# The per-layer gate of a one-layer encoder by Strassen's algorithm on token rows, with its weight operands kept on chip

## The chip, the cores and the metric

The kernel runs on one core of one Trainium2 chip. The metric is device time in microseconds (us) of that core: 2111.22 us before the change, the median of three runs that lie between 2110.23 and 2114.58 us.

## The reference

One layer of a streaming encoder, 2048 tokens of width 1024, all float32. The part that the change touches is the last two lines; `h` is the layer-normalised sum of input and token mixer, `p` a second input of width 256.

```
h = layer_norm(ALPHA * h + mix, ln1_g, ln1_b)
f = (silu(h @ ffn_w1) * (h @ ffn_w3)) @ ffn_w2          # width 2816
r = ALPHA * h + f
e = (p @ ple_w) * sigmoid(r @ ple_gate_w)               # "gate" and "ple"
out = layer_norm(r + e, ln2_g, ln2_b)
```

`ple_gate_w` is 1024 by 1024, `ple_w` is 256 by 1024, ALPHA is 2 to the power 1/4.

## The kernel before, in words

Every float32 product is made of three TensorE matmuls on operands cut in a high and a low part: `split` (L99 to L102) rounds a tile into its high part on ScalarE (ACT) and subtracts it for the low part on VectorE (DVE), and `mm3` (L122 to L125) issues high by high, high by low, low by high into one PSUM bank of 128 by 512. There are eight such banks, handed out in turn by `anybank`.

The stages follow one another: input projection, state-space scan and pooling, output projection and first layer norm (to about 519 us in the trace), then for each half `h` of the tokens (1024 tokens) `w13(h)`, which makes the SwiGLU's two products, and `w2_half(h)`, which makes `f` transposed, features on the partitions. At the end comes the gate over four blocks of 512 tokens, two in each half.

`w13` and `w2_half` use Strassen's algorithm in Winograd's form: a block product of 2 by 2 quadrants in seven products instead of eight. `weights7` (L770) loads two weight pieces, forms four sums on DVE and yields seven split operands one at a time; `next_w` (L819) takes them from a stream that runs five operands ahead (`LEAD`), over six buffers. The other side's seven operands are made once by `pieces7` (L823), written to DRAM (`Xv`, `Gv`) and read back by the GpSimd (POOL) queue into tiles that stay in SBUF (`xload1` for `w13(1)`, tile `xv`; `load_g` for `w2_half`, tile `gv`). `product` (L910) adds each of the seven into one of three banks, and the kernel reads a bank out between two products, by an ACT copy or a DVE add.

In `w2_half` the sums of six groups of such products collect in eight tiles `HR`: four copies by ACT in the first group (L1011), DVE adds elsewhere (L1012). After the last group ACT's queue writes them to DRAM as `Rr` (L1044), 16 transfers for each half.

The gate before does without Strassen. `prep_r` (L1047) reads `Rr` (tile `rr`) and `h` (tile `hn`, from `Hn`), adds ALPHA times `h` on DVE (L1056) and splits the sum into `rT`. `gate` does three of the four blocks with features on the partitions: for each of eight feature tiles two products for ple (bank `eb`) and eight for the gate (bank `ab`), with the weights streamed in and split for every block; `ln2` then transposes the result on TensorE (bank `vb`), normalises and writes it. The last block goes through `gate_rows`: tokens on the rows, the transposed `r` in `ro`, the same number of matmuls.

The program's order on each engine is fixed when the kernel is built: a scheduler walks the program by priority and hands out tile buffers as they come free, so instructions of neighbouring stages lie interleaved on an engine. Each engine then works its list strictly in order. DMAs are issued in order as well, from the lists of SP, ACT and POOL.

Of the kernel before, what the change touches and what calls it, by code (L numbers as in the profile page):

```python
# [40 lines left out]
def trunk_kernel(  # L41
# [125 lines left out]
    Gv = drp.tile([2, NF // 2, 7, 128, 1024], F32, name="Gv")  # L167
    Rr = drp.tile([2, 2, 128, 8, 512], F32, name="Rr")
# [599 lines left out]
    def weights7(src_a, src_b, pairs, sums=sums_x):  # L768
# [13 lines left out]
        a11, a12 = load(src_a)  # L782
        yield one(a11)
        a21, a22 = load(src_b)
# [189 lines left out]
    def w2_half(h):  # L974

        after = latest[0]
# [16 lines left out]
        for gi, pairs in W2:  # L993
# [53 lines left out]
    def prep_r(h, q):  # L1047

        rT[h][q], HR[h][q] = [], []
        for m2 in range(4):  # L1050
            t = slot([128, 2, 512], "rr")
            G.dma_start(t, Rr[h, q, :, 2 * m2:2 * m2 + 2])
            hn = sbig([128, 2, 512], "hn")
            for m in range(2):
                G.dma_start(hn[:, m], Hn[h, 2 * m2 + m, :, q])
            V.scalar_tensor_tensor(t, hn, ALPHA, t, MUL, ADD)  # L1056
            for m in range(2):
                HR[h][q].append(t[:, m])
                pr = pair("rT")
                split(pr[:, 0], pr[:, 1], t[:, m])  # L1060
                rT[h][q].append(pr)
            yield

    def prep_p(h, q):
        pr_ = xp.tile([128, 2, 512], F32, tag="x", name="pr_")
        SP.dma_start(pr_, pt[h, q].rearrange("p (k s) -> p k s", k=2))
        pT[h][q] = []
        for k in range(2):
            pr = pair("pT", sp)
            split(pr[:, 0], pr[:, 1], pr_[:, k])  # L1070
            pT[h][q].append(pr)

    def gate(h, q, banks=6):
        for m in range(8):
            if m % 4 == 0:
                ph, pl = weight(ple_w[m // 4], 2, 512)
            wh, wl = weight(gate_w[m], 8, 128)
            ms = slice(128 * (m % 4), 128 * (m % 4) + 128)
            ab, eb = anybank("ab", banks), anybank("eb", banks)
            for k in range(2):  # L1080
                mm3(eb, ph[:, k, ms], pl[:, k, ms], pT[h][q][k][:, 0], pT[h][q][k][:, 1], k == 0, k == 1)
            for k in range(8):
                mm3(ab, wh[:, k], wl[:, k], rT[h][q][k][:, 0], rT[h][q][k][:, 1], k == 0, k == 7)
            sg = evp.tile([128, 512], F32, tag="ev", name="sg")
            A.activation(sg, ab, AF.Sigmoid)
            V.tensor_tensor(sg, sg, eb, MUL)
            V.tensor_tensor(HR[h][q][m], HR[h][q][m], sg, ADD)
            yield

    def vtrans(b, h, q, t, m2):  # L1090
        for m in range(4):
            PE.transpose(b[:, m], HR[h][q][4 * m2 + m][:, 128 * t:128 * t + 128], ident)
        return b.rearrange("p a b -> p (a b)")


    ro = []

    def rows_r(h, q):

        two = slp.tile([128, 2, D], F32, tag="sl", name="ro")  # L1100
        ro.extend([two[:, 0], two[:, 1]] + [sbig([128, D], "ro") for _ in range(2)])
        for t in range(4):
            for m2 in range(2):
                A.copy(ro[t][:, 512 * m2:512 * m2 + 512], vtrans(tbank([128, 4, 128], "va"), h, q, t, m2))
            yield

    def weight2(src):

        raw = rawp[0].tile([128, 2, 512], F32, tag="wr", name="wr")
        SP.dma_start(raw, src.rearrange("p (k n) -> p k n", k=2))  # L1110
        wh, wl = pair("wh2"), pair("wl2")
        split(wh, wl, raw)
        return wh, wl

    def gate_rows(h, q):
        st = [sm.tile([128, 2, 6], F32, tag="st", name="st") for _ in range(4)]
        for n in range(2):
            ns = slice(512 * n, 512 * n + 512)
            acc = [bank([128, 512], "ab") for _ in range(4)]

            def part(t, us, kk0):
                cs = slice(128 * t, 128 * t + 128)
                for i, (wh, wl) in enumerate(us):
                    for k in range(2):
                        kt = 2 * (kk0 + i) + k
                        rp = rT[h][q][kt]
                        mm3(acc[t], rp[:, 0, cs], rp[:, 1, cs], wh[:, k], wl[:, k], kt == 0, kt == 7)

            for kk in range(2):
                u = weight(gate_r[n, kk], 2, 512)  # L1130
                for t in range(4):
                    part(t, [u], kk)
                yield
            ph, pl = weight2(ple_w[n])
            if n == 0:
                us = [weight(gate_r[n, kk], 2, 512) for kk in (2, 3)]
            else:
                us = [weight2(gate_r[n, kk]) for kk in (2, 3)]
            for t in range(4):
                cs = slice(128 * t, 128 * t + 128)  # L1140
                eb = side([128, 512], "eb")
                for k in range(2):
                    pp2 = pT[h][q][k]
                    mm3(eb, pp2[:, 0, cs], pp2[:, 1, cs], ph[:, k], pl[:, k], k == 0, k == 1)
                part(t, us, 2)
                sg = evp.tile([128, 512], F32, tag="ev", name="sg")
                A.activation(sg, acc[t], AF.Sigmoid)
                V.tensor_tensor(sg, sg, eb, MUL)
                V.tensor_tensor(ro[t][:, ns], ro[t][:, ns], sg, ADD)
                V.bn_stats(st[t][:, n], ro[t][:, ns])  # L1150
                if n == 1:
                    mv, rstd = ln_scale(st[t])
                    nb = sm.tile([128, 1], F32, tag="nb", name="nb")
                    V.scalar_tensor_tensor(nb, mv[:, 0:1], -1.0, rstd, MUL, MUL)
                    cut_at = CUTS[t]
                    o0, o1 = ro[t][:, 0:cut_at], ro[t][:, cut_at:D]
                    A.activation(o1, o1, AF.Identity, bias=nb, scale=rstd)
                    V.scalar_tensor_tensor(o0, o0, mv[:, 0:1], g2b[:, 0, 0:cut_at], SUB, MUL)
                    V.scalar_tensor_tensor(o0, o0, rstd, g2b[:, 1, 0:cut_at], MUL, ADD)
                    G.tensor_tensor(o1, o1, g2b[:, 0, cut_at:D], MUL)  # L1160
                    G.tensor_tensor(o1, o1, g2b[:, 1, cut_at:D], ADD)
                    SP.dma_start(ov[h, 4 * q + t, :, 0:cut_at], o0)
                    SP.dma_start(ov[h, 4 * q + t, :, cut_at:D], o1)
                yield

    def ln2(h, q):
        for t in range(4):
            bs = [vtrans(tbank([128, 4, 128], "vb"), h, q, t, m2) for m2 in range(2)]
            mv, rstd = ln_stats(bs)
            o = xp.tile([128, D], F32, tag="x", name="o")  # L1170
            for m2 in range(2):
                ms = slice(512 * m2, 512 * m2 + 512)
                V.scalar_tensor_tensor(o[:, ms], bs[m2], mv[:, 0:1], g2b[:, 0, ms], SUB, MUL)
            V.scalar_tensor_tensor(o, o, rstd, g2b[:, 1], MUL, ADD)
            G.dma_start(ov[h, 4 * q + t], o)
            yield
# [41 lines left out]
    rT, HR, pT = ([[None, None], [None, None]] for _ in range(3))  # L1218

# [24 lines left out]
    drive(w13(1), None, 0)  # L1244
    drive(w2_half(1), None, 0)
    mid_pools.close()
    rawp[0] = ctx.enter_context(tc.tile_pool(name="wrq", bufs=2, reuse_waits="tile"))
    g2b = slp.tile([128, 2, D], F32, tag="sl", name="g2b")
    G.dma_start(g2b[:, 0], ln2_g.broadcast_to([128, D]))
# [81 lines left out]
```

## Time and profile before

| What | Value |
|---|---|
| median of three runs | 2111.22 us |
| the profiled execution, its own time | 2113.13 us |
| its span, first to last instruction | 2111.4 us |
| mean granted TensorE clock | 0.987 |
| PE (matmul) busy | 2031.3 us, 96% |
| DVE busy | 1582.4 us, 75% |
| ACT busy | 858.1 us, 41% |
| POOL busy | 333.1 us, 16% |

The span is 1.7 us shorter than the execution's own time, and that execution is 1.9 us above the median. Matmuls overlap each other in the record, so a single one is recorded longer than the step from one to the next; the cost of one more matmul is read from a stretch in which TensorE never waits, as time by count. Idle time of an engine that is not the bottleneck costs nothing. In the trace's lists "idle before" an instruction names what released it.

### The profile page before, as it was taken

Reading aid. Unit: us, or ns where it says so; the run is one execution under the profiler, and the core shown is the slowest. Engines: PE = TensorE matmul, PEld = TensorE weight load, DVE = VectorE, ACT = ScalarE, POOL = GpSimd, SP = SyncE. Lnnn points to the kernel's source line nnn. Section 1 sums busy time; section 2 is a strip of 40 time slices with the busy share of each in tenths; the row PEclk is TensorE's granted clock in tenths of the full one; section 3 lists DMA queues with packets and bytes.
Section 4 is the critical chain, followed back from the end, with each engine's and each line's share of the span. In section 5 each row is a group of like instructions: output and inputs, shape, how many; then the busy total and the mean of one; then the engine's idle time right before and its main releaser. Section 6 shows DMA issues by size and latency. Waiting matters only on the chain.

```text
span 2111.4 us, 25700 instructions
## 1 busy us (share of the span) xinstructions
PE 2031.3 (96%) x9064; PEld 1644.9 (78%) x9064; DVE 1582.4 (75%) x2812; ACT 858.1 (41%) x1453; POOL 333.1 (16%) x603
## 2 busy tenths in 40 slices
PE   9999899999899999999999999999999899979997
PEld 7877678777688778887788888888888688758886
DVE  7599699668688786666788867767766588866877
ACT  4533645644555454344222244444434322142341
POOL 2012101110111111013211100101103221111113
PEclk9999999999999999999999999999999999989999
DMA  7636757766656654349766833434438876354542
GB/s 250 219 119 210 275 169 235 233 213 216 219 211 245 246 216 165 124 176 398 284 248 227 301 140 134 171 134 150 169 130 342 315 262 237 129 220 148 207 164 100
DMA packets 149184, 440.82 MB, mean 209 GB/s; under 512 B 15344, under 2 KB 41552, under 8 KB 149056
## 3 DMA queue, kind: packets, MB, share of 16 engines
q0 software_dynamic: 72160, 258.80, 32.9%
q1 hardware_dynamic: 42912, 148.92, 20.2%
q10 hardware_dynamic: 33984, 31.46, 4.3%
q8 instruction: 71, 1.16, 0.2%
q14 instruction: 57, 0.47, 0.1%
HBM read 292.88 MB, written 148.34 MB: 209 GB/s over the span
## 4 chain that ended last, share of the span: by engine, by line
PE 71%; DMA 10%; issue 7%; DVE 7%; ACT 3%; POOL 2%; SPq 0%; POOLq 0%; ACTq 0%; DVEq 0%
PE fb L123 12%; PE fb L125 12%; PE fb L124 12%; PE f L123 6%; PE f L125 6%; PE f L124 6%; PE ab L123 2%; PE ab L124 2%; PE ib L125 2%; PE ab L125 2%; PE ib L123 2%; PE ib L124 2%; DMA hl<-Hd 1%; DMA gv<-Gv 1%; DMA Hd<-ze 1%
## 5 line engine op out<-in xcount | busy, mean ns | idle before, releaser
L123 PE MATMUL fb<-xv,wv 128*128 128x512 f32 x1232 | 482.2, 396 | 6.4 <-ACT u L961 4.5
L124 PE MATMUL fb<-xv,wv 128*128 128x512 f32 x1232 | 486.0, 394 | 0.0
L125 PE MATMUL fb<-xv,wv 128*128 128x512 f32 x1232 | 482.3, 395 | 0.2 <-DVE wv L102 0.2
L101 ACT CAST wv<-ws 128x512 fp32r<-128x512 f32 x264 | 163.6, 620 | 379.1 <-PE fb L125 179.9
L123 PEld LDWEIGHTS fb<-xv,wv 128*128 128x128 f32 x1232 | 232.3, 189 | 61.3 <-ACT u L961 6.1
L125 PEld LDWEIGHTS fb<-xv,wv 128*128 128x128 f32 x1232 | 232.1, 188 | 54.6 <-DVE wv L102 0.6
L124 PEld LDWEIGHTS fb<-xv,wv 128*128 128x128 f32 x1232 | 232.5, 189 | 53.0
L123 PE MATMUL f<-gv,wv 128*128 128x512 f32 x616 | 242.3, 397 | 15.9 <-ACT HR L1011 13.6
L1012 DVE TENSOR_TENSOR HR<-HR,f 128x512 f32<-128x512 f32 x304 | 202.7, 684 | 60.2 <-PE f L125 56.5
L124 PE MATMUL f<-gv,wv 128*128 128x512 f32 x616 | 243.5, 395 | 0.0
L102 DVE TENSOR_TENSOR wv<-ws,wv 128x512 fp32r<-128x512 f32 x264 | 181.6, 688 | 81.8 <-ACT wv L101 81.4
L125 PE MATMUL f<-gv,wv 128*128 128x512 f32 x616 | 235.5, 395 | 0.0
L101 ACT CAST wh<-wr 128x1024 fp32r<-128x1024 f32 (+1 forms) x102 | 101.6, 999 | 219.3 <-PE ab L124 73.7
L831 POOL DMA_DIRECT2D Gv<-xo x154 | 82.7, 537 | 660.7 <-DVE xo L102 625.6
L102 DVE TENSOR_TENSOR wl<-wr,wh 128x1024 fp32r<-128x1024 f32 (+1 forms) x102 | 117.8, 1158 | 71.0 <-ACT wh L101 70.9
L101 ACT CAST wv<-wq 128x512 fp32r<-128x512 f32 x198 | 122.5, 621 | 90.0 <-PE f L125 65.3
L102 DVE TENSOR_TENSOR wv<-wq,wv 128x512 fp32r<-128x512 f32 x198 | 136.0, 687 | 30.2 <-ACT wv L101 29.1
L123 PEld LDWEIGHTS f<-gv,wv 128*128 128x128 f32 x616 | 116.6, 189 | 45.7 <-ACT HR L1011 14.9
L124 PEld LDWEIGHTS f<-gv,wv 128*128 128x128 f32 x616 | 116.7, 189 | 26.5
L125 PEld LDWEIGHTS f<-gv,wv 128*128 128x128 f32 x616 | 116.4, 189 | 26.9
L989 POOL DMA_DIRECT2D gv<-Gv x154 | 81.6, 531 | 230.2 <-PE f L125 187.8
L101 ACT CAST xo<-tt 128x512 fp32r<-128x512 f32 x104 | 64.6, 621 | 111.7 <-DVE tt L844 62.4
(316 smaller groups left out, 3563.4 us busy)
## 6 DMA issues: line engine op xcount, KB each, us to landing
Gv<-xo POOLq DMA_DIRECT2D x154, 512.0 KB, 3.1
gv<-Gv POOLq DMA_DIRECT2D x154, 512.0 KB, 7.5
wq<-in_w_dram SPq DMA_DIRECT2D x132, 512.0 KB, 4.2
wr<-in_w_out_dram SPq DMA_DIRECT2D x32, 512.0 KB, 4.4
Xv<-xo POOLq DMA_DIRECT2D x28, 512.0 KB, 3.8
xv<-Xv POOLq DMA_DIRECT2D x28, 512.0 KB, 5.9
wr<-in_gate_w_dram SPq DMA_DIRECT2D x24, 512.0 KB, 4.0
pre<-in_x_dram SPq DMA_DIRECT2D x16, 512.0 KB, 5.7
```

What stands on the lines that cost most here:

```text
L101: A.copy(hi, src)
L102: V.tensor_tensor(lo, src, hi.bitcast(F32), SUB)
L123: PE.matmul(ps, ah, bh, start=first, stop=False, **kw)
L124: PE.matmul(ps, ah, bl, start=False, stop=False, **kw)
L125: PE.matmul(ps, al, bh, start=False, stop=last, **kw)
L831: G.dma_start(dst[i], v.bitcast(F32).rearrange("p a n -> p (a n)"))
L989: G.dma_start(v.bitcast(F32).rearrange("p a n -> p (a n)"), Gv[h, pi, i])
L1012: return V.tensor_tensor(o, o, bank, ADD)
```

## The change

The gate is done by Strassen for all tokens, as eight pairs of 128-token tiles (`PAIRS`), tokens on the rows.

- `w2_half` reads `h` (tile `hl`) from SP's queue and adds ALPHA times it to `HR[um]` on DVE, once for each of the eight tiles, in groups 1 to 4 of the six (two in each). `Rr` then holds `r` itself, and `prep_r` goes.
- `wprep` runs beside `w13(1)`: it loads `gate_r` (eight SP transfers, tile `gw`), forms the seven operands of the gate's weights with `pieces7` and writes them to `Wv`. `wload` reads all 28 back on POOL's queue after `w2_half(1)`'s last weight load, into the places that `xv` had (`GW`).
- `rows7(n)` loads `r` of pair `n` (tile `r2`, 1 MB, from SP's queue; pair 0 in two halves) and yields its seven split operands through the same stream as the FFN's weights, by `seven`, the part of `weights7` behind its loads.
- `gate(n)`: seven products of four `mm3` each into three banks; between them `rows` transposes `r2` (bank `va`) into `ro`, and `done` makes ple's product (bank `eb`, weights `ple` kept on chip), sigmoid, product, sum and the statistics; `norm` normalises and writes each tile.
- `gate_rows`, `ln2`, `rows_r`, `prep_p`, `weight2` go.

```diff
@@ weights7 / seven
+        a11, a12 = load(src_a)
+        a21, a22 = load(src_b)
+        yield from seven(a11, a12, a21, a22, pairs, sums)
+
+    def seven(a11, a12, a21, a22, pairs, sums):
...
@@ all_weights
+        for n in range(len(PAIRS)):
+            yield from rows7(n)
@@ w2_half
+                else:
+                    um = per_units[gi] + mu
+                    if um < 8:
+                        hl = xp.tile([128, 2, 512], F32, tag="x", name="hl")
+                        with tc.issue_after(latest[0].ins):
+                            SP.dma_start(hl, Hn[h, um])
+                        V.scalar_tensor_tensor(hr[um], hl, ALPHA, hr[um], MUL, ADD)
...
-    def prep_r(h, q):
...
-    def gate(h, q, banks=6):
...
-    def gate_rows(h, q):
...
-    def ln2(h, q):
...
+    def wprep():
+        for k in range(4):
+            two = []
+            for kt in (k, k + 4):
+                t = sbig([128, 2, 512], "gw")
+                SP.dma_start(t, gate_r[:, kt // 2, :, 512 * (kt % 2):512 * (kt % 2) + 512].rearrange("n p c -> p n c"))
+                two.append(t)
+                yield
+            lo, hi = two
+            yield from pieces7(lo[:, 0], lo[:, 1], hi[:, 0], hi[:, 1], Wv[:, k])
...
+    def wload(after):
+        with tc.issue_after(after.ins):
+            for i in range(7):
+                for k in range(4):
+                    v = GW[i][k] = xplace(i, "gw")
+                    G.dma_start(v.bitcast(F32).rearrange("p a n -> p (a n)"), Wv[i, k])
+
+    PAIRS = [(h, q, tp) for h in range(2) for q in range(2) for tp in range(2)]
+    rs = {}
+
+    def rows7(n):
+
+        h, q, tp = PAIRS[n]
+        ts_ = slice(256 * tp, 256 * tp + 256)
+        if n == 0:
+            lo, hi = (xp.tile([128, 4, 256], F32, tag="x", name="r2") for _ in range(2))
+            with tc.issue_after(latest[0].ins):
+                SP.dma_start(lo, Rr[h, q, :, 0:4, ts_])
+                SP.dma_start(hi, Rr[h, q, :, 4:8, ts_])
+        else:
+            t = slp.tile([128, 8, 256], F32, tag="sl", name="r2")
+            SP.dma_start(t, Rr[h, q, :, :, ts_])
+            lo, hi = t[:, 0:4], t[:, 4:8]
+        rs[n] = lo, hi
+        (a11, a21), (a12, a22) = ([x_[:, :, 128 * c:128 * c + 128] for c in range(2)] for x_ in (lo, hi))
+        yield from seven(a11, a12, a21, a22, 4, sums_b if n == 0 else sums_x)
...
+    def gate(n):
...
+        pv = operand(sp, "s", "pT").rearrange("p a (k s) -> p a k s", k=2)
+        split(pv[:, 0], pv[:, 1], praw)
+        r2 = rs.pop(n)
...
+        def rows(c):
+
+            ro[c] = xp.tile([128, D], F32, tag="x", name="ro")
             for m2 in range(2):
+                b = anybank("va")
+                for m in range(4):
+                    PE.transpose(b[:, 128 * m:128 * m + 128], r2[m2][:, m, 128 * c:128 * c + 128], ident)
+                A.copy(ro[c][:, 512 * m2:512 * m2 + 512], b)
+
+        def done(c, nn, t, bk):
+            eb = anybank("eb")
+            for k in range(2):
+                cs = slice(128 * c, 128 * c + 128)
+                w = ple[2 * nn + k]
+                mm3(eb, pv[:, 0, k, cs], pv[:, 1, k, cs], w[:, 0], w[:, 1], k == 0, k == 1)
...
+                V.tensor_tensor(t, t, bk, ADD)
+                A.activation(t, t, AF.Sigmoid)
+            V.tensor_tensor(t, t, eb, MUL)
+            o = ro[c][:, 512 * nn:512 * nn + 512]
+            V.tensor_tensor(o, o, t, ADD)
+            V.bn_stats(st[c][:, nn], o)
+
+        def norm(c):
...
+            V.scalar_tensor_tensor(o[:, :at], o[:, :at], mv[:, 0:1], g2[:, :at], SUB, MUL)
+            V.scalar_tensor_tensor(o[:, :at], o[:, :at], rstd, b2[:, :at], MUL, ADD)
+            SP.dma_start(dst[:, :at], o[:, :at])
...
+        for i in range(7):
+            wv = next_w()
+            product(i, banks, 4, lambda k: tile_of(wv, k), lambda k: (GW[i][k][:, 0], GW[i][k][:, 1]))
+            if i == 0:
+                e = evp.tile([128, 512], F32, tag="ev", name="e")
+                A.copy(e, banks[0])
+                rows(0)
+            elif i == 1:
+                done(0, 0, e, banks[1])
+            elif i == 2:
+                u2 = evp.tile([128, 512], F32, tag="ev", name="u2")
+                A.copy(u2, banks[0])
+                rows(1)
...
@@ program
-    drive(w13(1), None, 0)
+    drive(w13(1), wprep(), 0.5)
     drive(w2_half(1), None, 0)
+    wload(latest[0])
     mid_pools.close()
...
+    gate_consts()
+    for n in range(len(PAIRS)):
+        gate(n)
```

How the change moves instructions is shown at two places. The first is the hand-over from `w2_half(1)` to the gate. On PE before, behind the last `w2_half` products (banks `f`):

```order
L124 MATMUL f_15030<-gv,wv 128x512
L125 MATMUL f_15030<-gv,wv 128x512
L123 MATMUL ab<-rT,wh 128x512
L123 MATMUL eb<-pT,wh 128x512
L124 MATMUL eb<-pT,wh 128x512
L125 MATMUL eb<-pT,wl 128x512
```

On PE now, some 45 rows ahead of the last `f` product (`gw` are the gate's weight operands, `wv` those of pair 0's `r`):

```order
L123 MATMUL ab<-gw,wv 128x512
L123 MATMUL f_15151<-gv,wv 128x512
L124 MATMUL f_15151<-gv,wv 128x512
L125 MATMUL f_15151<-gv,wv 128x512
L124 MATMUL ab<-gw,wv 128x512
L123 MATMUL f_15251<-gv,wv 128x512
L124 MATMUL f_15251<-gv,wv 128x512
L125 MATMUL f_15251<-gv,wv 128x512
L123 MATMUL ab<-gw,wv 128x512
```

Before, the first gate product stood behind every product of `w2_half(1)`. Now 24 of pair 0's gate matmuls stand ahead of the last of them, 24 more follow it directly, and ple's first six (bank `eb`) come behind those.

On ACT before, at the same hand-over, the last writes of `Rr`, then casts of `prep_r`'s tiles:

```order
L1044 DMA Rr<-HR 128x512 x2
L101 CAST wh<-wr 128x1024
L1044 DMA Rr<-HR 128x512 x6
L101 CAST wh<-wr 128x1024
L101 CAST rT<-rr 128x512 x10
```

On ACT now (`r_15469` is pair 1's `r2`; `u_15486` and `d_15516` are tiles `u2` and `d5` of pair 0):

```order
L101 CAST pT<-praw 128x512
L1058 DMA Rr<-HR 128x512
L101 CAST wv<-r_15469 128x512
L1058 DMA Rr<-HR 128x512 x2
L1182 COPY u_15486<-ab 128x512
L101 CAST wv<-r_15469 128x512
L1186 COPY d_15516<-ab 128x512
L1135 COPY ro<-va 128x512 x4
```

The cast of pair 1's `r2`, whose load waits for an `HR` buffer, now stands ahead of the copy that empties pair 0's first bank.

The second place is a middle group of `w2_half(1)`. On DVE before, adds into `HR` between the splits and sums of other stages:

```order
L102 TENSOR_TENSOR xo<-tt,xo 128x512
L1012 TENSOR_TENSOR HR<-HR,f_13773 128x512
L844 TENSOR_TENSOR tt<-g 128x512
L1012 TENSOR_TENSOR HR<-HR,f_13776 128x512
L1012 TENSOR_TENSOR HR<-HR,f_13627 128x512
L1012 TENSOR_TENSOR HR<-HR,f_13625 128x512
```

On DVE now:

```order
L850 TENSOR_TENSOR tt<-g 128x512
L1026 TENSOR_TENSOR HR<-HR,f_13800 128x512
L1026 TENSOR_TENSOR HR<-HR,f_13798 128x512
L102 TENSOR_TENSOR xo<-tt,xo 128x512
L1016 SCALAR_TENSOR_TENSOR HR<-hl,HR 128x1024
L1026 TENSOR_TENSOR HR<-HR,f_13949 128x512
```

One pass over 1024 columns has come in between two adds; there are eight in each half.

## Rows read from the trace of the kernel before

**Rows 1.** The page, busy time of each engine, then the chain by engine.
```profile
PE 2031.3 (96%) x9064; PEld 1644.9 (78%) x9064; DVE 1582.4 (75%) x2812; ACT 858.1 (41%) x1453; POOL 333.1 (16%) x603
...
PE 71%; DMA 10%; issue 7%; DVE 7%; ACT 3%; POOL 2%; SPq 0%; POOLq 0%; ACTq 0%; DVEq 0%
```

**Rows 2.** Windows: from:to, its length, busy us (instructions), granted clock, DMA share, GB/s.
```profile
560.00:942.00 382.00, 380.93 (x1638) 308.02 (x1637) 287.45 (x462) 181.24 (x325) 55.94 (x105) 1.00 0.53 196
1170.00:1210.00 40.00, 40.00 (x174) 32.44 (x173) 32.65 (x54) 11.33 (x19) 5.83 (x11) 1.00 0.89 323
1210.00:1622.00 412.00, 412.00 (x1790) 335.87 (x1789) 282.85 (x453) 181.28 (x327) 47.78 (x90) 1.00 0.43 161
1700.00:1845.00 145.00, 145.00 (x629) 117.89 (x629) 121.51 (x191) 31.45 (x50) 21.67 (x41) 1.00 0.56 204
1845.00:1900.00 55.00, 40.59 (x155) 31.21 (x154) 34.23 (x43) 21.15 (x31) 8.65 (x17) 0.88 0.61 228
1900.00:2000.00 100.00, 99.18 (x457) 81.36 (x456) 71.94 (x101) 28.98 (x40) 14.81 (x27) 1.00 0.50 174
2000.00:2098.00 98.00, 98.00 (x466) 80.30 (x465) 77.37 (x113) 33.10 (x48) 15.15 (x22) 1.00 0.38 140
```

**Rows 3.** Waits of PE from 1840 us on: total us, times, longest.
```profile
PE ab L123 <- ACT rT L101: 10.2, 2, 9.7
PE eb L123 <- ACT sg L1085: 2.6, 1, 2.6
PE ab L123 <- ACT wh L101: 1.3, 2, 0.8
PE ab L124 <- DVE rT L102: 1.2, 1, 1.2
```

**Rows 4.** Groups by line; the gate's matmuls, first of three lines for each kind.
```profile
L123 PE MATMUL ab<-rT,wh 128*128 128x512 f32 x192 | 77.2, 404 | 11.5 <-ACT rT L101 10.2 <-ACT wh L101 1.3
L123 PE MATMUL ab<-wh,rT 128*128 128x512 f32 x64 | 25.7, 402 | 0.0
L123 PE MATMUL eb<-pT,wh 128*128 128x512 f32 x48 | 19.7, 410 | 2.6 <-ACT sg L1085 2.6
L123 PE MATMUL eb<-wh,pT 128*128 128x512 f32 x16 | 6.4, 399 | 0.0
```

**Rows 5.** Timeline of PE just behind the wait of 9.72 us: start, duration.
```profile
1855.14 0.79 PE L123 MATMUL ab<-rT,wh 128*128 128x512 f32 x1 [9.72 <-ACT rT L101]
...
1858.29 0.63 PE L123 MATMUL ab<-rT,wh 128*128 128x512 f32 x1
1858.71 0.63 PE L124 MATMUL ab<-rT,wh 128*128 128x512 f32 x1
```

**Rows 6.** Groups by line: DVE's and ACT's work of the kinds that move.
```profile
L1056 DVE SCALAR_TENSOR_TENSOR rr<-hn,rr 128x1024 f32<-128x1024 f32 x16 | 19.3, 1220 | 10.7 <-issue 8.7 <-DMA hn<-Hn 2.0
L1174 DVE SCALAR_TENSOR_TENSOR o<-o,mv,g2b 128x1024 f32<-128x1024 f32 x12 | 15.4, 1282 | 0.7
L101 ACT CAST rT<-rr 128x512 fp32r<-128x512 f32 x32 | 18.3, 619 | 23.3 <-DVE rr L1056 23.2
```

**Rows 7.** Timeline of DVE in `w2_half(1)`, back-to-back instructions of 512 columns.
```profile
1667.52 0.68 DVE L790 TENSOR_TENSOR ws<-wq 128x512 f32<-128x512 f32 x1
1668.12 0.68 DVE L792 TENSOR_TENSOR ws<-wq,ws 128x512 f32<-128x512 f32 x1
1668.72 0.68 DVE L102 TENSOR_TENSOR wv<-ws,wv 128x512 fp32r<-128x512 f32 x1
1669.32 0.68 DVE L1012 TENSOR_TENSOR HR<-HR,f 128x512 f32<-128x512 f32 x1
```

**Rows 8.** DMA issues: queue, count, KB each, median us to landing.
```profile
Rr<-HR ACTq DMA_DIRECT2D x32, 256.0 KB, 6.2
rr<-Rr POOLq DMA_DIRECT2D x16, 512.0 KB, 6.4
```

**Rows 9.** Timeline of ACT at the hand-over; ACTq is its DMA issues.
```profile
1831.72 5.93 ACTq L1044 DMA_DIRECT2D Rr<-HR  x5
...
1842.10 4.45 ACTq L1044 DMA_DIRECT2D Rr<-HR  x6
1849.70 1.04 ACT L101 CAST wh<-wr 128x1024 fp32r<-128x1024 f32 x1 [8.84 <-DMA Rr<-HR]
```

**Rows 10.** Timeline of PE, the last matmul.
```profile
2098.54 0.40 PE L125 MATMUL ab<-wh,rT 128*128 128x512 f32 x1
```

**Rows 11.** Timeline of DVE at the end, last tile's product and last normalisation.
```profile
2100.80 0.68 DVE L1148 TENSOR_TENSOR sg<-sg,eb 128x512 f32<-128x512 f32 x1
...
2106.20 1.01 DVE L1159 SCALAR_TENSOR_TENSOR ro<-ro,mv,g2b 128x768 f32<-128x768 f32 x1
```

More of the change, by code (lines that the diff above doesn't have):

```diff
@@ L974, in w2_half @@
     def w2_half(h):
+        per_units = [2 * gi - 2 for gi in range(len(W2))]
         after = latest[0]
@@ L1045, in w2_half @@
                 yield
-    def prep_r(h, q):
[L1049 to L1071, printed above, removed]
-    def gate(h, q, banks=6):
[L1074 to L1079, printed above, removed]
-            for k in range(2):
[L1081 to L1102, printed above, removed]
-            for m2 in range(2):
-                A.copy(ro[t][:, 512 * m2:512 * m2 + 512], vtrans(tbank([128, 4, 128], "va"), h, q, t, m2))
-            yield
@@ L1107, in weight2 @@
[L1107 to L1113, printed above, removed]
-    def gate_rows(h, q):
[L1116 to L1136, printed above, removed]
-            else:
[L1138 to L1164, printed above, removed]
@@ new lines, in trunk_kernel @@
+    GW = [[None] * 4 for _ in range(7)]
+    def wload(after):
[21 more added lines that the diff above has]
+        yield from seven(a11, a12, a21, a22, 4, sums_b if n == 0 else sums_x)
@@ new lines, in trunk_kernel, with gate_consts @@
+    ple, gb = [], [None]
+    def gate_consts():
+        gb[0] = gcp.tile([128, 2, D], F32, tag="g2", name="g2b")
+        for n in range(2):
+            raw = xp.tile([128, 2, 512], F32, tag="x", name="raw")
+            SP.dma_start(raw, ple_w[n].rearrange("p (k n) -> p k n", k=2))
+            for k in range(2):
+                v = operand(sp, "s", "ple") if n + k == 0 else operand(plp, "pl", "ple")
+                split(v[:, 0], v[:, 1], raw[:, k])
+                ple.append(v)
+        G.dma_start(gb[0][:, 0], ln2_g.broadcast_to([128, D]))
+        G.dma_start(gb[0][:, 1], ln2_b.broadcast_to([128, D]))
@@ new lines, in gate @@
+    def gate(n):
+        h, q, tp = PAIRS[n]
+        ts_ = slice(256 * tp, 256 * tp + 256)
+        praw = evp.tile([128, 2, 256], F32, tag="ev", name="praw")
+        SP.dma_start(praw, pt[h, q].rearrange("p (k s) -> p k s", k=2)[:, :, ts_])
+        pv = operand(sp, "s", "pT").rearrange("p a (k s) -> p a k s", k=2)
+        split(pv[:, 0], pv[:, 1], praw)
+        r2 = rs.pop(n)
+        ro, st = [None, None], [sm.tile([128, 2, 6], F32, tag="st", name="st") for _ in range(2)]
+        banks = [anybank("ab") for _ in range(3)]
+        def rows(c):
+            ro[c] = xp.tile([128, D], F32, tag="x", name="ro")
+            for m2 in range(2):
+                b = anybank("va")
[8 more added lines that the diff above has]
+                mm3(eb, pv[:, 0, k, cs], pv[:, 1, k, cs], w[:, 0], w[:, 1], k == 0, k == 1)
+            if t is None:
+                t = evp.tile([128, 512], F32, tag="ev", name="sg")
+                A.activation(t, bk, AF.Sigmoid)
+            else:
+                V.tensor_tensor(t, t, bk, ADD)
[5 more added lines that the diff above has]
+        def norm(c):
+            o, g2, b2 = ro[c], gb[0][:, 0], gb[0][:, 1]
+            mv, rstd = ln_scale(st[c])
+            dst = ov[h, 4 * q + 2 * tp + c]
+            at = CUTS[2 + c] if n == len(PAIRS) - 1 else D
+            if at < D:
+                nb = sm.tile([128, 1], F32, tag="nb", name="nb")
+                V.scalar_tensor_tensor(nb, mv[:, 0:1], -1.0, rstd, MUL, MUL)
+                A.activation(o[:, at:], o[:, at:], AF.Identity, bias=nb, scale=rstd)
+            V.scalar_tensor_tensor(o[:, :at], o[:, :at], mv[:, 0:1], g2[:, :at], SUB, MUL)
+            V.scalar_tensor_tensor(o[:, :at], o[:, :at], rstd, b2[:, :at], MUL, ADD)
+            SP.dma_start(dst[:, :at], o[:, :at])
+            if at < D:
+                G.tensor_tensor(o[:, at:], o[:, at:], g2[:, at:], MUL)
+                G.tensor_tensor(o[:, at:], o[:, at:], b2[:, at:], ADD)
+                SP.dma_start(dst[:, at:], o[:, at:])
+        for i in range(7):
[11 more added lines that the diff above has]
+                rows(1)
+            elif i == 3:
+                d5 = evp.tile([128, 512], F32, tag="ev", name="d5")
+                A.copy(d5, banks[2])
+            elif i == 4:
+                done(1, 1, d5, banks[0])
+            elif i == 5:
+                done(0, 1, u2, banks[2])
+                norm(0)
+            else:
+                done(1, 0, None, banks[0])
+                norm(1)
```

29 lines of the change are left out of this document (3 added, 26 removed).

## The prediction

> **What bounds the kernel now.** I read the page first: PE is busy for 96% of the span and holds 71% of the chain that ended last, DVE is next with 75% [rows 1]. So matmuls count, and waits of PE; work of other engines counts only where PE ends up waiting for it. Then the windows by stage. Through `w13(1)` and most of `w2_half(1)` PE is busy all the time (412.00 of 412.00 us, 145.00 of 145.00), and again through the last 98 us of the gate; only the 55 us behind 1845 us stand out, with PE busy for 40.59 us and a granted clock of 0.88 [rows 2]. That is the hand-over from `w2_half(1)` to the gate. The list of PE's waits there tells why: 10.2 us for the casts of `rT`, which wait for `Rr` and `h` to be read back, then 2.6, 1.3 and 1.2 us [rows 3].
>
> **What one matmul costs.** Durations overlap, so I take time by count where PE never waits: 145.00 us / 629 = 0.2305 us [rows 2]. The groups' 0.40 us [rows 4] would price it 1.7 times too high. *The Trainium skill, "TensorE: Matmul & The Clock Gate", Part 1, gives 215.7 ns from start to start for back-to-back matmuls of 512 columns at full clock. By that estimate the 96 matmuls below are worth 20.7 us instead of 22.1; the trace, where each matmul has a weight load of its own, differs, and its 0.2305 us decides.*
>
> **The matmuls removed.** Before, the gate has (192 + 64) x 3 = 768 products in `ab` and (48 + 16) x 3 = 192 in `eb` [rows 4], 960 in all. Now it is 8 pairs x 7 products x 4 x 3 = 672 and 8 x 4 x 2 x 3 = 192, 864 in all. Transposes stay at 128. 96 x 0.2305 = 22.1 us less, straight off the chain, since PE sets the pace.
>
> **The hand-over.** 155 instructions in the 55 us would take 35.5 us by 0.2305 (I take a transpose at a full step, one or two tenths of a us in all): 19.5 us are lost there, 14.4 of them idle and 5.1 to a low clock [rows 2]. Behind the wait of 9.72 us matmuls start 0.42 us apart, the 1.2 GHz level [rows 5]. What follows now? Pair 0's `r` belongs to half 0 and has long been written, its weights' operands come in by `wload` just as `xload1` brings those of `w13(1)`, and 24 of its matmuls stand ahead of the last `f` products. The nearest row is that older hand-over, `w2_half(0)` to `w13(1)`: PE busy for 40.00 of 40.00 us beside DMA at 0.89 [rows 2]. So the low bound for what is left is 0, the high one the old 19.5 us. I do not take 0, for one chain is new: pair 1's `r2` needs an `HR` buffer, so ACT's write of `Rr` must have landed. The first eight writes of the half are out by 1837.7 [rows 9], 6.2 us later they land [rows 8], about 1844; `r2` is 1 MB where a read of 512 KB took 6.4 us, so it lands at 1850 to 1853; the cast behind it takes 0.6. ACT works in order, and behind that cast stands the copy of pair 0's bank (`u_15486`), without which product 4 cannot start. PE arrives there after 24 matmuls, six of ple and eight transposes, some 7.7 us behind 1845.3, so at 1853. That is 0 to 3 us of waiting, with a low clock behind it (5.1 / 14.4 = 0.35 us for each us idle). The `ro` copies need buffers that `HR` holds until its last write lands (issued at 1842 to 1846.5 [rows 9], landed near 1853), again near PE's time. I take 5 us, so -19.5 + 5 = -14.5.
>
> **ALPHA h in `w2_half`.** 16 passes of 1.22 us on DVE [rows 6] move from the gate into groups 1 to 4. What hides them is DVE's slack: a weight unit there has 84 matmuls, 19.4 us of PE, against 14 adds, 7 splits and 4 sums, 25 DVE steps. Back to back they start 0.60 us apart [rows 7], 15.0 us, and 16.2 with the new pass; by their recorded 0.68 us it is 18.2, still under 19.4. The `hl` loads go to SP's queue five operands ahead, and reads of that size landed in 6.4 us [rows 8], so DVE should not be held by them; queued behind a late one would be the adds that free PE's banks. Nothing is gained (low bound 0); if all lay on the path it would be 19.5. The row nearest is the stage itself, with no wait at 84% DVE. I take 1 us.
>
> **`wprep` in `w13(1)`.** 28 splits and 20 differences, 48 x 0.60 = 28.8 us of DVE, 28 casts x 0.62 = 17.4 us of ACT, 28 writes to DRAM. `w13(0)` carries exactly such a load beside it (`xprep1`, eight more passes on top), and PE was busy there for 380.93 of 382.00 us [rows 2]. So 0 to 1.1 us; the new part is that the eight `gw` loads stand in SP's queue ahead of weights, where `xprep1`'s were on POOL's. I take 1 us.
>
> **The gate's own pace.** A pair costs PE 108 x 0.2305 = 24.9 us and 1.6 us for 16 transposes. DVE has 27 steps of 512 columns (7 splits, 4 sums, 1 split of `p`, 3 bank adds, 4 products, 4 adds, 4 statistics), 16.2 us at 0.60, four passes of 1024 at 1.28 [rows 6] and small ones of 0.7: 22.0 of 26.5 us, 83%; by recorded durations 24.4, 92%. PE had no wait in the old gate's last 98 us with DVE at 79% [rows 2]. New and narrow are one buffer for `pT`, three for `e`, `u2`, `d5`, and `eb` sharing the eight banks with the three that a pair holds. From 0.8 us (the idle in 1900 to 2000 [rows 2]) to 8 x (2.6 + 0.9) = 28, if every pair pays one wait such as that for `sg` [rows 3] with its low clock. I take 3 us. ple's weights, split once now instead of eight times, lie beside it all.
>
> **The end.** Before, the last tile's product starts 2.3 us behind the start of the last matmul, as DVE was behind [rows 10, 11]. Now the sigmoid runs beside ple's six matmuls and DVE has no weights left to split; what follows is the same chain. -1 us, between -2 and +1.
>
> **The sum.** -22.1 - 14.5 + 1 + 1 + 3 - 1 = -32.6 us, against the span of 2111.4: 2078.8. The profiled execution took 2113.13, 1.7 more than its span, and is 1.9 above the median of the three runs; against the median of 2111.22 it is 2078.6, and I say 2079.
>
> **Rivals.**
> *The hand-over keeps its loss.* What speaks for it is the new chain through `HR`, `Rr` and `r2`, and the old row in which a cast waited 8.84 us for writes of `Rr` [rows 9]. Against: `w13(1)`'s start. Then only the matmuls go: 2079 + 14.5 = 2093. *The Trainium skill, "DMA: Bandwidth & Descriptors", under "Issuing engines are not separate DMA queues", says that DMAs from several engines run on the same 16 DMA engines and interleave. It speaks against the change: `r2` on SP's queue would not pass `wload`'s 14 MB on POOL's. By the rule this rival's time holds. The trace agrees so far as DMA share was already 0.89 in the older hand-over.*
> *DVE or the banks hold PE in every pair*, as bounded above: 28 us in place of 3, 2104. For it speaks DVE's 83 to 92%, against it `w2_half` at 84% without a wait.
> *Slower: SP's queue is late with `r2`.* Outputs, `praw` and `r2` share one list, and an output waits for its norm. If `r2` of pairs 1 to 7 were read only when the pair before is done, each would begin with a read of 6.4 us, a cast of 0.62 and a subtraction of 0.69, 7.7 us idle and 2.7 of low clock: 7 x 10.4 = 73 us, less the 3 counted, 2149. It decides from (32.6 + 3) / 7 = 5.1 us for each pair. Against it: `r2` has two buffers, so a read can stand a pair ahead.
> That the work isn't cut is no rival: the program has 864 such matmuls.
>
> **How the numbers follow.** Forecast 0.62, with a range of its own of 2068 to 2092 (hand-over and pace at their low bounds: -22.1 - 19.5 - 2 + 0.8 = -43; pace at half its bound: +11); hand-over kept 0.20; DVE or banks 0.10; SP's queue 0.05; something else 0.03. The range of 2066 to 2104 reaches from 2 us below the low bounds (each is a small remainder, good to some tenths) to the second rival. A measurement can tell 0.2%, 4.2 us, from no change. Faster by more than that: 0.62 + 0.20 + 0.09 = 0.91; within it 0.03; slower 0.06.
>
> **What would show it.** Right: 864 matmuls in `ab` and `eb`; PE's waits between the last `f` product and the gate's end under 10 us in sum, clock 1.00 there; no new waits of PE in `w13(1)` and in groups 1 to 4. Wrong: a PE wait of many us on casts from `r2` or copies into `ro` just behind the hand-over (first rival); waits of a few us in each pair on DVE's adds or on `pT` (second); waits on DMA `r2` that recur every 30 us (third). The forecast fails if these come to more than 25 us together.

## The result, and the profile after

The changed kernel takes 2085.36 us (median of 4 runs, 2084.70 to 2089.64), the kernel before beside it 2111.77 us: a ratio of 0.9878, 95% interval 0.9861 to 0.9895, 26.4 us less. The forecast was 2079 us, 32.6 less. The profiled execution took 2085.38 us with a span of 2083.6, 27.8 under the 2111.4 of before.

The page, as in [rows 1]: busy time by engine, and the chain that ended last.

```profile
PE 2008.1 (96%) x8968; PEld 1626.0 (78%) x8968; DVE 1611.5 (77%) x2886; ACT 876.8 (42%) x1515; POOL 337.0 (16%) x595
PE 54%; issue 20%; DMA 12%; DVE 7%; POOL 4%; ACT 3%; POOLq 0%; SPq 0%; ACTq 0%; DVEq 0%
```

PE lost the 96 matmuls (9064 to 8968), DVE's share rose by two points, and PE, busy for 96%, is still the bound. The chain that ended last runs another way here (PE 54%, "issue" 20%, against 71% and 7%); I did not follow that up. The gate's groups of matmuls, against [rows 4]: the counts of `ab` and `eb` on one of three lines.

```profile
L123 PE MATMUL ab<-gw,wv 128*128 128x512 f32 x224 | 89.9, 404 | 2.4 <-ACT u L1182 2.4
L123 PE MATMUL eb<-ple,pT 128*128 128x512 f32 x64 | 25.5, 398 | 0.0
```

Three lines each make 672 and 192. The windows, with the columns of [rows 2]:

```profile
1170.00:1210.00 40.00, 40.00 (x174) 32.39 (x173) 34.63 (x59) 12.21 (x21) 6.70 (x13) 1.00 0.98 349
1210.00:1622.00 412.00, 411.84 (x1787) 335.14 (x1786) 305.61 (x490) 197.28 (x355) 60.56 (x114) 1.00 0.55 202
1700.00:1845.00 145.00, 144.99 (x632) 117.88 (x631) 128.06 (x201) 31.82 (x52) 29.05 (x55) 1.00 0.79 287
1845.00:1900.00 55.00, 52.59 (x236) 42.49 (x235) 40.07 (x64) 23.43 (x41) 5.34 (x7) 0.97 0.57 200
1900.00:1950.00 50.00, 50.00 (x234) 40.81 (x234) 43.33 (x69) 20.40 (x37) 5.82 (x4) 1.00 0.28 95
1950.00:2000.00 50.00, 50.00 (x235) 40.90 (x234) 44.81 (x70) 21.40 (x38) 6.42 (x4) 1.00 0.23 73
2000.00:2050.00 50.00, 50.00 (x234) 40.97 (x234) 38.19 (x61) 19.06 (x34) 7.03 (x4) 1.00 0.17 65
```

DVE carries 22.8 us more beside `w13(1)` and 6.6 more in the window of `w2_half(1)`, and PE is as full there as before. The 55 us of the hand-over now have PE busy for 52.59 us at a clock of 0.97 (40.59 at 0.88 before), and the gate behind them is full. The list of PE's waits from 1840 us to the end is one row long, where [rows 3] had four, 15.3 us in all:

```profile
PE ab L123 <- ACT u L1182: 2.4, 1, 2.4
```

So where are the missing 6 us? Behind the last matmul. It ends at 2064.6, and the span at 2083.6: 19 us, where it was 12.4 before (2098.9 to 2111.3). The end's timeline on POOL and SP's queue (start, duration):

```profile
2072.86 0.72 POOL L1168 TENSOR_TENSOR ro<-ro,g2b 128x256 f32<-128x256 f32 x1
2073.61 0.33 SPq L1169 DMA_DIRECT2D out_dram<-ro  x1
```

The last store is issued 9.0 us behind the last matmul (9.7 before), and nothing works after it. But the program's closing instructions have rows of their own, under the line that ends the kernel (durations in ns, least, median, longest; first and last start):

```profile
L1335 POOLq DRAIN  x3: 46/97/10000, 2072.8 to 2083.3; - x3
L1335 SPq DRAIN  x3: 7/7/7, 2075.4 to 2083.1; - x3
```

A DRAIN is an instruction with which an engine closes its program. SP's comes at 2075.4, when the last store has landed. POOL's takes 10.00 us and ends at 2082.82; the other engines' last rows all start behind it, at 2083.0 or later. The same two rows of the kernel before:

```profile
L1326 POOLq DRAIN  x3: 46/98/1670, 2107.8 to 2111.1; - x3
L1326 SPq DRAIN  x3: 7/7/7, 2110.5 to 2110.8; - x3
```

There it took 1.67 us and was done ahead of SP's at 2110.5. In the changed kernel that is 7.3 us (2082.8 less 2075.5) lost to a closing instruction of an engine with 16% of work.

### The profile page after: what moved, and what is told of

Read it like the earlier page. It is cut to its first block, busy times and chain, and to the rows that moved or that the text cites. A ratio compares the mean times of both kernels' runs of the same rounds, so it can differ in the third digit from the quotient of the medians.

```text
span 2083.6 us, 25684 instructions
## 1 busy us (share of the span) xinstructions
PE 2008.1 (96%) x8968; PEld 1626.0 (78%) x8968; DVE 1611.5 (77%) x2886; ACT 876.8 (42%) x1515; POOL 337.0 (16%) x595
## 3 DMA queue, kind: packets, MB, share of 16 engines
q0 software_dynamic: 73632, 265.10, 34.1%
## 4 chain that ended last, share of the span: by engine, by line
PE 54%; issue 20%; DMA 12%; DVE 7%; POOL 4%; ACT 3%; POOLq 0%; SPq 0%; ACTq 0%; DVEq 0%
PE f L123 6%; PE f L124 6%; PE f L125 6%; PE fb L123 6%; PE fb L125 5%; PE fb L124 5%; PE ab L123 2%; PE ab L124 2%; PE ab L125 2%; DMA Gv<-xo 2%; PE ib L125 2%; PE ib L123 2%; PE ib L124 2%; POOL Gv L837 2%; DMA hl<-Hd 2%
## 5 line engine op out<-in xcount | busy, mean ns | idle before, releaser
L101 ACT CAST wv<-ws 128x512 fp32r<-128x512 f32 x296 | 183.3, 620 | 384.1 <-PE f L125 170.5
L102 DVE TENSOR_TENSOR wv<-ws,wv 128x512 fp32r<-128x512 f32 x296 | 202.9, 686 | 68.3 <-ACT wv L101 67.9
L101 ACT CAST xo<-tt 128x512 fp32r<-128x512 f32 x120 | 74.6, 621 | 120.1 <-DMA Gv<-xo 49.2
L102 DVE TENSOR_TENSOR xo<-tt,xo 128x512 fp32r<-128x512 f32 x120 | 82.3, 686 | 40.1 <-ACT xo L101 39.5
L123 PE MATMUL ob<-wh,mx 128*128 128x512 f32 x256 | 102.3, 409 | 7.4 <-ACT sg L681 7.4
```

The costliest lines, as they stand in the source:

```text
L101: A.copy(hi, src)
L102: V.tensor_tensor(lo, src, hi.bitcast(F32), SUB)
L123: PE.matmul(ps, ah, bh, start=first, stop=False, **kw)
```

## The experiments

Two questions: do the matmuls and the half-0-first order carry the gain, as the prediction has it, and what makes POOL's drain long? The executions of one kernel on one chip lie 5 to 14 us apart (run 2: 2083.97 to 2098.01), and in the profiled executions the part ahead of the first w1/w3 matmul, which the change does not touch, differs by up to 9.7 us. So I read stages and the tail from each trace, and the times only where they are far apart.

**Which part of the tail?** Run 1 sends both small pieces of the last pair through POOL's queue (the expectation names only the very last; the line serves both).

```
-                SP.dma_start(dst[:, at:], o[:, at:])
+                G.dma_start(dst[:, at:], o[:, at:])
```

> The very last store (256 columns of the last tile, 128 KB) is issued from POOL's queue instead of SP's; all else as in the changed kernel. In the changed kernel POOL's closing DRAIN took 10.00 us (1.67 us before the change) and the program's end waited for it: 19.0 us from the last matmul to the end against 12.5. Theory A, the drain is long because POOL's own last DMA issue lies 220 us back (24 us back before the change): the drain falls to 2 to 3 us, the end comes 11 to 13 us behind the last matmul, 2078 to 2080 us. Theory B, it follows from where POOL's program ends and not from its queue: the drain stays near 10 us and the time at 2084 to 2088. Theory C, the drain waits for the multiply and add that POOL does just ahead of it: as under B.

Measured: ratio 0.9842 (0.9812 to 0.9871). The drain:

```profile
L1335 POOLq DRAIN  x3: 51/98/2397, 2079.0 to 2082.2; - x3
```

It fell to 2.4 us, but POOL's second issue came 2.9 us behind its last operation, so the end is 15.2 us behind the last matmul. Theory B is out, and theory A looked right.

Run 2 gives POOL one store 22 us ahead of its drain, about where the kernel before had its last:

```
-            SP.dma_start(dst[:, :at], o[:, :at])
+            (G if n == len(PAIRS) - 2 and c == 1 else SP).dma_start(dst[:, :at], o[:, :at])
```

> The second tile of the last pair but one is stored from POOL's queue instead of SP's, some 28 us ahead of the end, which is about where the kernel before had its last POOL issue (24 us). Nothing in the last pair is touched. Theory A (time since POOL's last DMA issue): the drain falls to 2 to 3 us, 2077 to 2080 us. Theories B and C: the drain stays near 10 us, 2084 to 2087 us.

Run 3 takes POOL's multiply and add out of the tail (`CUTS = (640, 640, 1024, 1024)`):

> The last pair's rows are no longer cut: VectorE does all 1024 columns, ScalarE's and POOL's parts go, and POOL's last arithmetic is the pow of one column. The chain behind the last matmul grows by 384 and 256 columns on VectorE, about 0.4 us for the last tile by the 1.01 us that 768 columns took, twice over. Theory C (the drain waits for POOL's long multiply and add): the drain falls under 3 us, 2078 to 2081 us. Theories A and B: it stays near 10 us and, as POOL is done about 2.4 us sooner, ends sooner by that: 2082 to 2085 us.

Runs 2 and 3, in this order:

```profile
L1335 POOLq DRAIN  x3: 46/98/10080, 2079.2 to 2089.8; - x3
```

```profile
L1335 POOLq DRAIN  x3: 46/98/10720, 2078.9 to 2090.1; - x3
```

The drain stays long in both (ratios 0.9887 and 0.9862): theory A in the form "a DMA 22 us ahead", and theory C, both fall. In run 3 the drain begins 0.7 us sooner relative to POOL's last operation and still ends 9.24 us behind it, to the hundredth what the changed kernel has; as that operation comes sooner, the end lies 16.5 us behind the last matmul instead of 19.0, about the 2.4 us named for that case.

Run 5 gives POOL only the first tile's small piece, 1.8 us ahead of the drain:

```
+                (G if c == 0 else SP).dma_start(dst[:, at:], o[:, at:])
```

> Of the last pair only the 384-column piece of the first tile is stored from POOL's queue (the run before that had both small pieces there, and its drain took 2.4 us); every other store is SP's. Theory A, POOL's drain is long unless POOL issued a DMA within the last few us: the drain falls to 1 to 3 us, and as the last store stays with SP the end comes 11 to 12 us behind the last matmul instead of 19. Theory D, it was the issue as POOL's very last instruction that cut it short: the drain stays near 10 us, the end 19 us behind the last matmul. Theory E, POOL had stood idle for 16 us ahead of its last arithmetic (6 us at most in the kernel before), and the drain pays for it: stays near 10 us.

Run 6 keeps POOL awake with four one-column multiplies behind results of the last pair (`tick`, a `G.tensor_tensor` into a scratch tile):

> Four one-column multiplies into a scratch tile are put on POOL in the last pair, each behind a result of that pair, so that POOL is never idle for over about 6 us in its last 30 us; it issues no DMA later than in the changed kernel. Theory E (idle time ahead of the tail): the drain falls to 1 to 3 us, 2077 to 2080 us on a chip where the changed kernel takes 2085. Theory A (no DMA issued by POOL of late): the drain stays near 10 us.

Run 7 is the kernel before with one edit:

```
-            G.dma_start(ov[h, 4 * q + t], o)
+            SP.dma_start(ov[h, 4 * q + t], o)
```

> The kernel before with one edit: the 12 stores of its row-form norm beside the gate are issued from SP's queue instead of POOL's, so POOL's last DMA issue lies more than 60 us before the end instead of 21. POOL's arithmetic stays as it was, with no idle time over about 7 us. Theory A: POOL's drain rises from 1.67 to about 10 us and the time by 7 to 8 us, 2118 to 2124 us. Theory E: the drain stays under 3 us and the time within 3 us of the kernel before.

Their drains, run 5, 6 and 7:

```profile
L1335 POOLq DRAIN  x3: 46/98/10082, 2081.6 to 2092.1; - x3
```

```profile
L1344 POOLq DRAIN  x3: 46/98/10000, 2070.9 to 2081.4; - x3
```

```profile
L1326 POOLq DRAIN  x3: 46/98/9347, 2115.0 to 2124.9; - x3
```

Run 5 ends theory A: a DMA 1.8 us ahead of the drain leaves it at 10.08 us. Run 6 ends theory E. Run 7 reproduces the loss in the old kernel: 2124.60 against 2118.37 us, ratio 1.0022 (1.0007 to 1.0037), the end 19.0 us behind the last matmul instead of 12.4. Theory A had forecast that too, but run 5 speaks against it. So the loss does not need Strassen's gate; it comes with fewer stores on POOL's queue. Set side by side, the drains follow the number of DMAs that POOL issued in the whole program. That made theory F, tested by runs 9, 11 and 12: the first two move loads of the gate's weights, issued between 1206 and 1362 us in the traces, and so 720 to 870 us ahead of the end.

```
 def wprep():
-                SP.dma_start(t, gate_r[:, kt // 2, ...
+                (G if k == 0 else SP).dma_start(t, gate_r[:, kt // 2, ...      # run 9
+                G.dma_start(t, gate_r[:, kt // 2, ...                           # run 11
```

> Two of the eight loads that the gate's weights' preparation issues beside the second w1/w3 stage go from SP's queue to POOL's, 400 us ahead of the end; nothing of the tail is touched. POOL then issues 545 DMAs in the whole program, against 543. Theory F, from the runs so far: behind POOL's last operation its drain takes 8.59 us with 535 DMAs issued, 9.24 with 543, 9.32 with 544 (0.081 us for each), but 0.91 with 547, wherever they stood, so something is worked off at the end for each DMA issued since a point that moves between 544 and 545. Then the drain ends 0.7 to 1 us behind POOL's last operation, the end comes 11 to 12 us behind the last matmul, and the time is 7 to 8 us under the changed kernel's. Theory G, what counts is POOL's DMAs in the last 60 us: the drain stays near 10 us and the time at the changed kernel's.

> All eight of those loads go to POOL's queue, 551 DMAs. Theory F: the drain ends 0.91 + 4 x 0.081 = 1.23 us behind POOL's last operation (547 gave 0.91), still ahead of the wait for the last store, so the time is that of the run with two. Theory G: near 9.9 us.

> The changed kernel itself, unedited, so that its time, its stages and its drain stand beside those of the other kernels on one chip: the drain 10.0 us again under every theory, the gate's pairs as before, the time 1.2% under the kernel before.

Runs 9, 11 and 10:

```profile
L1335 POOLq DRAIN  x3: 46/97/1750, 2076.2 to 2079.8; - x3
```

```profile
L1335 POOLq DRAIN  x3: 46/98/2648, 2076.2 to 2079.3; - x3
```

```profile
L1335 POOLq DRAIN  x3: 46/98/9997, 2081.6 to 2092.2; - x3
```

POOL's DMAs counted in each trace, and how far behind POOL's last operation its drain ends (start plus duration of the one less start plus duration of the other):

| kernel | POOL's DMAs | last one ahead of the drain, us | drain ends behind last operation, us | span's end behind last matmul, us |
|---|---|---|---|---|
| run 12 | 515 | 220 | 6.95 | 16.7 |
| run 7 (before, edited) | 535 | 94 | 8.59 | 19.0 |
| changed; runs 3, 4, 6, 8, 10 | 543 | 207 to 232 | 9.24 | 16.5 to 19.0 |
| run 2; run 5 | 544 | 22; 2 | 9.32 | 19.1 |
| run 9 | 545 | 214 | 0.99 | 12.1 |
| run 1 | 545 | 0 | 5.25 | 15.2 |
| before | 547 | 21 | 0.91 | 12.4 |
| run 11 | 551 | 219 | 1.89 | 11.6 |

From 515 to 544 each DMA more costs 0.081 us at the end: run 12 was forecast at 6.97 and came to 6.95. With two more than the changed kernel's 543, issued 870 us ahead of the end (and not the 400 us of the expectation), it drops to 0.99. That ends theory G, and theory D too: no issue stands at POOL's end there. Up to 544 neither the time of the last DMA nor what POOL does in the tail orders the drains. Nor do the packets on the queue of POOL's DMAs (72160 in the kernel before with its short drain, 73632 in the changed kernel, 73920 in run 9), nor SP's issues (305 in run 3 with its long drain and in run 9). Run 11 shows the limit of the law: 1.23 was expected and 1.89 came, so behind the drop the slope isn't the same; its time, 2084.83 us, is that of run 9, as expected. Run 1 is apart as well: there the 545th issue lies in the tail itself, and part of the work seems to be done there, which no run shows.

Run 9 is also the version that beats both kernels: 2085.86 us where the changed kernel (run 10) took 2093.59 on that chip, 7.7 less, with no overlap of the single times (2082.18 to 2089.38, and 2090.30 to 2095.14). The ratios to the kernel before are 0.9855 (0.9833 to 0.9877) and 0.9890 (0.9871 to 0.9909); their intervals overlap by little. In the profiled executions the end comes 12.1 us behind the last matmul instead of 19.0.

**Do the matmuls set the gate's pace?** Run 4 repeats one product of each pair:

```
+            for _ in range(2 if i == 1 else 1):
                 product(i, banks, 4, ...
```

> Each of the eight pairs issues its second product (12 matmuls) twice over; the repeat starts its bank afresh, so the result is the same. That is 96 matmuls more, as many as the change took away. Theory 1, the matmul sets the pace of the gate: 96 x 0.2305 us = 22.1 us more than the changed kernel, 2106 to 2109 us. Theory 2, VectorE, the banks or the operands' landings hold the pairs: much of the added work is filled in, under 10 us more, 2085 to 2095 us.

Two windows of run 4, columns as above:

```profile
1900.00:1950.00 50.00, 50.00 (x235) 41.07 (x234) 39.77 (x60) 18.80 (x34) 5.82 (x4) 1.00 0.26 90
1950.00:2000.00 50.00, 50.00 (x231) 40.88 (x230) 41.06 (x62) 18.22 (x32) 5.81 (x4) 1.00 0.20 71
```

PE is full. From the first `ab` matmul of pair 1 to that of pair 7 it takes 177.5 us against 161.1 in the changed kernel: 16.4 us for 72 matmuls, 0.228 each. Theory 1 holds there. In all, w13(1)'s last matmul to the gate's last, 456.4 us against 439.7, only 16.8 of the 22 came out. Pair 0's 12 went into time that the hand-over wastes anyway: pair 0 grew by 0.2 us, what stands ahead of it shrank by 1.1, and the wait of 2.4 is gone. Pair 7's 12 made it and the end only 1.3 us longer; why is open. The median, 2105.46 us (ratio 0.9949, where runs 2 and 3, with the same drain, average 0.9875 there: 15.8 us), agrees.

**What is half 0 first worth?** Run 8 takes the pairs of half 1 first, and so has to begin the gate's operand stream behind `w2_half(1)`; the two can't be told apart in it:

```
-    PAIRS = [(h, q, tp) for h in range(2) ...
+    PAIRS = [(h, q, tp) for h in (1, 0) ...
-        for n in range(len(PAIRS)):        # in all_weights
-            yield from rows7(n)
+    stream[0] = chain(*[rows7(n) for n in range(len(PAIRS))])     # behind w2_half(1)
+    for _ in range(LEAD):
+        more()
```

> The eight pairs are taken with half 1 first, and the gate's operand stream is begun only behind the second half of w2, so that the first pair's residual is the one stored last. The sums are the same. Theory 1 (the prediction's step: reading the half stored long ago is what removes the hand-over): TensorE stands behind its last w2 matmul for the landing of the last stores (6.2 to 6.6 us), that of the read (6.6 us), the first split and the slow clock behind it, 15 to 20 us more than the changed kernel, 2100 to 2106 us where that takes 2085. Theory 2 (the hand-over was hidden by the gate's operands kept on the chip, whichever half comes first): under 5 us more.

Its only wait of PE from 1830 us on, the read that ends it, and the window around it:

```profile
PE va L1132 <- DMA r<-Rr: 13.1, 1, 13.1
```

```profile
1848.23 0.38 SPq L1091 DMA_DIRECT2D r<-Rr  x1
1858.75 1.12 PE L1132 MATMUL va<-ident,r 128*128 128x128 f32 x4 [13.06 <-DMA r<-Rr]
```

```profile
1840.00:1860.00 20.00, 6.87 (x28) 5.03 (x27) 6.64 (x11) 0.72 (x2) 2.64 (x5) 0.70 0.88 318
```

The wait is the one that theory 1 named, and its sum fits (13.1 us where 6.2 + 6.6 = 12.8), but not its parts: PE ends its last w2 matmul at 1845.7, the read is issued 2.5 us later, and its data are there 10.5 us behind the issue. From the first w1/w3 matmul to the last of the gate it takes 1558.4 us; nine kernels with the gate as changed take 1544.9 to 1551.5, mean 1547.1, so it costs 11.3 us and not 15 to 20: the slow clock behind it lasts only for some 2 us of matmuls, and the changed kernel's own hand-over loss, 4 us, went with it. In the medians, 2095.46 against 2091.77 and 2090.86 of runs 5 and 6, it shows as 4 us only, inside the scatter.

**What do the two added steps cost?** Run 12 leaves them out:

```
-                        with tc.issue_after(latest[0].ins):
-                            SP.dma_start(hl, Hn[h, um])
-                        V.scalar_tensor_tensor(hr[um], hl, ALPHA, hr[um], MUL, ADD)
-    drive(w13(1), wprep(), 0.5)
+    drive(w13(1), None, 0)
```

> The changed kernel without its two added steps: the eight Hn loads with their ALPHA h passes in each w2 half, and the preparation of the gate's seven weights' operands beside w1/w3 of half 1. Left out of the result: the ALPHA h residual, and the gate's weights (other stored tiles of the same size are loaded in their place). The prediction has each at +1 us. Theory 1: from the first w1/w3 matmul to the last w2 matmul 2 us less than the changed kernel. Theory 2 (a part of VectorE's 24 us more comes out on TensorE's path): 5 to 20 us less. The 28 stores of the preparation are POOL's, so POOL issues 515 DMAs: theory F has the drain end 9.24 - 28 x 0.081 = 6.97 us behind its last operation, which takes another 2.3 us off the end; theory G leaves it at 9.24.

```profile
L1332 POOLq DRAIN  x3: 46/98/7712, 2071.5 to 2079.7; - x3
```

From the first w1/w3 matmul to the first of `ab` it takes 1321.3 us; the nine kernels above take 1321.3 to 1327.5, mean 1324.0. That would be 2.8 us for the two steps, at the edge of the scatter. But the stretch holds `w13(0)`, which neither step touches, and which was 2 us slower than the mean in run 12. Leaving it out, from the last w1/w3 matmul of half 0 to the last of half 1, run 12 takes 648.2 us and the nine kernels 650.6 to 655.5, mean 652.7; the kernel before and run 7, which have neither step, take 647.8 and 648.0. That is 4.5 us, clear of the scatter. From there to the first of `ab` nothing shows: 216.0 against a mean of 216.3. So the steps cost 4 to 5 us, twice theory 1's 2 and just under theory 2's 5 to 20. `w2_half(1)`, where the ALPHA h passes stand as in `w2_half(0)`, shows no loss, so most of it is probably `wprep`'s; no run leaves out one of the two alone. The time of run 12, 2084.28 us, has the shorter drain in it too.

## Why the prediction came out as it did

Direction, range and the main mechanism were right; 6 us of the gain are missing by the medians, 4.8 in the profiled executions (27.8 where 32.6 was forecast), and the end accounts for more than that. By its own steps, in the profiled executions:

| step | forecast, us | measured, us |
|---|---|---|
| matmuls removed | -22.1 | -21.9 (96 x 0.228, run 4) |
| hand-over | -14.5 | -15.5 (4.0 us kept) |
| ALPHA h, `wprep` | +2 | +2.5 (run 12: 4.5) |
| the gate's pace | +3 | +1.6, none of it a wait |
| the end | -1 | +6.5 |

With 1.0 us less ahead of the first w1/w3 matmul these make the 27.8.

- *Matmuls.* The counts and the price by start-to-start distance held. The rule of the Trainium skill weighed there ("TensorE: Matmul & The Clock Gate", Part 1, 215.7 ns from start to start) would make 72 matmuls 15.5 us; run 4 shows 16.4.
- *The hand-over.* The one wait left is the one named, product 4 behind the copy `u_15486` behind pair 1's cast behind the read of its `r2`:

```profile
1848.88 0.54 SPq L1097 DMA_DIRECT2D r<-Rr  x1
1861.64 0.62 ACT L101 CAST wv<-r 128x512 fp32r<-128x512 f32 x1 [5.80 <-DMA r<-Rr]
1862.56 0.59 ACT L1182 COPY u<-ab 128x512 f32<-128x512 f32 x1 [0.30 <-issue]
1863.19 0.79 PE L123 MATMUL ab<-gw,wv 128*128 128x512 f32 x1 [2.42 <-ACT u L1182]
```

  With its clock it costs 4.0 us: pair 0 takes 33.4 us here, and 29.4 in run 9, where there was no wait in the gate at all. 5 us were forecast. That the size came out is partly luck. The forecast set a landing of `r2` at 1850 to 1853 against PE's arrival at 1853; in the trace `r2` is issued at 1848.9 and there only at 1861.6, 12.7 us later, and PE, with 24 gate matmuls ahead of the last `f` product, arrives at 1860.8. Both were forecast some 8 us or more too early, and only their difference held. The clock over the 55 us was 0.97 and not the 1.00 of the forecast's signs. The DMA share was 1.01 from 1848 to 1862; that this made the read late isn't tested. Over the profiled executions the wait varies between 0 and 4.5 us. Run 8 shows the other side, what the first pair pays when its residual isn't long stored.
- *ALPHA h and `wprep`.* DVE's slack hid most of them: by the forecast's prices DVE has 46 us more to do in these stages (16 passes of 1.22 us, 44 steps of 0.60), and 2.5 us came out here, 4.5 by run 12. That is more than the 1.1 us that the forecast set as `wprep`'s high bound if `wprep` is where it lies. (The 44 steps are 28 splits and 16 differences; the forecast counted 20 differences and had 28.8 us in place of 26.4.)
- *The gate's pace.* From last `f` product to last matmul the gate went from 253.7 to 217.9 us (the 24 `ab` matmuls and 4 transposes ahead of that product counted to the gate), -35.8. Taking -21.9 and -15.5 from it leaves +1.6. No rival on DVE, the banks or SP's queue came true: PE had no wait behind pair 0. (The range of its own should end at 2090 by its sum, 2079 + 11, and not at 2092; the measured time lies within either.)
- *The end* is the step that failed. "What follows is the same chain" was right as far as it went: the last store is issued 0.7 us sooner. The step stopped at the last store and left out what closes the program. POOL's queue lost 60 DMAs (32 reads of `Hn`, 16 of `Rr`, 12 stores) and got 56 (28 writes and 28 reads of `Wv`), by the trace's count 543 in place of 547. With 544 and fewer the drain was long in every run, with 547, and in runs 9 and 11 with 545 and 551, short: it ends 9.24 us behind POOL's last operation instead of 0.91. Run 7 makes the loss in the old kernel, run 9 takes it out of the new one. Without the 6.5 us the profiled execution would have gained 34.3, 1.7 more than the forecast; measured on its own chip, run 9 gains 28.4 us of medians where the changed kernel (run 10) gains 20.7.

What stays open: what POOL works off in its drain, why the step lies between 544 and 545 DMAs in these programs, the slope behind it, and which of the two added steps costs the 4.5 us.

## What to carry to other kernels

Price a removed matmul by the distance of starts in a stretch without waits: that held here to a microsecond. Check that the engine that takes over its work has slack in that very stage, but leave a few us for it: of 46 us given to VectorE 2.5 to 4.5 came out. Reading first what was stored long ago was worth 11 us here. And read the trace to the last instruction, not to the last store: moving DMAs from POOL's queue changed its closing cost by 8 us here, and moving two loads, 870 us ahead of the end, took that back.

## What the runs showed of the hardware

POOL's closing DRAIN took 1.7 to 10.7 us, by the number of DMAs that POOL had issued in the program: 0.081 us for each from 515 to 544 (6.95, 8.59, 9.24 and 9.32 us behind its last operation), then 0.99 at 545, 0.91 at 547 and 1.89 at 551. When the last had been issued, 218, 22 or 2 us ahead of the drain, changed nothing in runs 3, 2 and 5; only in run 1, with its 545th issue at the drain itself, was it 5.25 us. What the engine does in that time no run shows.
